# Another order of the first stage, a pool's mean ahead of a scheduling point, and one preparation step behind a product

## The chip, the cores and the metric

The kernel runs on one core of one Trainium2 chip. The metric is the time of one execution in microseconds, measured on the device; lower is better. Three executions of the kernel before took 1081.11, 1081.81 and 1083.24 us, a median of 1081.81 us.

## The reference

One layer of a hybrid decoder block on x of 1024 tokens by 1024 channels, all in float32: an RMSNorm, one projection `h @ w_in` whose columns are the queries and keys of four heads of differential attention, their values v, a multiscale trailing mean ("pool") and a gated short convolution; the output projection with a residual; then a second RMSNorm, a SwiGLU feed-forward layer of 2816 hidden channels with a residual, and a last RMSNorm.

```python
h = rmsnorm(x, g_mix[l]);  proj = h @ w_in[l]
q, k, v, p, gb, gc, hin = jnp.split(proj, list(split_pts), axis=-1)
att = diff_attention(q1, q2, k1, k2, vh, rel_bias, lam)
att = rmsnorm(att, subln_g[l], SUBLN_EPS) * (1.0 - lam_init)
pool = multiscale_pool(p, w_pool[l], pool_scale[l])
conv = short_gated_conv(gb, gc, hin, conv_w[l])
x = x + (jnp.concatenate([att, pool, conv], axis=-1) @ w_o[l])
h = rmsnorm(x, g_ffn[l])
x = x + (jax.nn.silu(h @ w_gate[l]) * (h @ w_up[l])) @ w_down[l]
return rmsnorm(x, g_final)
```

The multiscale pool is, per group of 64 channels, the mean over the last 2, 4, 8 or 16 tokens minus the token itself, times a small matrix.

## The kernel before

Every product is done in three passes of a split number: ACT writes a rounded high half (`nc.scalar.copy`), DVE the rest (`tensor_sub`), and PE multiplies high by high, low by high and high by low (`PASSES`). So nearly every operand passes through ACT and then DVE before PE can use it (`split_exact` L48, `halves_of` L136).

The tokens are worked in two halves, c = 0 and c = 1, of 512. The **first stage** (L186 to L379) loads x transposed, in four tiles of 256 channels for each half, and the weights of v, of k and of q. For c = 0 it does not wait for the norm: h is x times the gain, and the factor 1/rms of a token ("rstd") is put on behind the products. That factor comes from `squares` (ACT, L231), `square_sum` (DVE adds them, and for the last tile splits the total into two halves, L235), `token_rstd` (eight small PE products against ones, L255; a DVE step L259, a GpSimd power L261 and a DVE copy `rep` L263) and `along` (four PE transposes L269 and an ACT copy, `rbc`). `v_out` (L198) takes v of a block of 128 tokens from PSUM with rstd on it: twice an ACT step (L209) and a DVE step (L210). For c = 1, `normalise` (L275) makes the true h: DVE multiplies (`hn`, L288), then the two halves are split off (L50, L51). PE then does the products of v for c = 1 (`v_products`, L226). `of_gained` (L338) are the products of k and of q for c = 0, 24 matmuls each.

In this stage and in two others the program's text sets the order of the instructions on PE, ACT, DVE and GpSimd (`manual_schedule`); elsewhere a scheduler orders them, and may fill PE's order with products of the next part (L560: k and q for c = 1). Each engine takes its instructions in that order, and an instruction that waits holds up all behind it. PSUM banks come from three tags with two banks each: v of c = 0 has "c" and "f"; q's products take the "f" bank that `v_out(0, 2)` empties, and the v products of c = 1 need both "c" banks, emptied by `v_out(0, 0)` and `v_out(0, 1)`.

After this, `chain` (L530) runs the other columns of `w_in` while attention is worked between them. The pool's part is a generator, `windows` (L489): sums over windows, two `yield`s, the mean and its halves `ph` and `pl`, a `yield`, and the products (L523). At each `yield` other work is put in.

In the feed-forward layer, `unit(m, name)` (L1064) is one of seven products of a fast 2 by 2 scheme; M6, M7 and M4 add into one bank of the tag "f", which DVE reads in between (L1085, L1087, L1096). `prepare(m, part)` (L864) readies weights: part 1 is four DVE sums (L876 to L879).

Of the kernel before, what the change touches and what calls it, by code (L numbers as in the profile page):

```python
# [71 lines left out]
def tile_hybrid_block(ctx, tc, x, g_mix, w_in, lq1, lk1, lq2, lk2, subln_g, rel_bias, w_pool,  # L72
# [50 lines left out]
    def bank(tag, shape=(P, 512)):  # L123
        return psp.tile(list(shape), F32, tag=tag, name="ps_" + tag)
# [11 lines left out]
    def halves_of(raw, shape, pin=False, eng=nc.vector):  # L136

        hi = sl.new("w_hi", shape, F32R)
        lo = sl.new("w_lo", shape, F32R)
        ins = nc.scalar.copy(hi, raw)  # L140
        if pin:
            tc.keep_in_program_order(ins)
        eng.tensor_sub(lo, raw, hi.bitcast(F32))  # L143
        sl.done(raw)
        return hi, lo
# [76 lines left out]
    def v_products(c, n, ps, tbs=range(4)):  # L222
        w = wv[n // 2]
        for tb in tbs:
            for j, (a, b) in enumerate(PASSES):
                ins = nc.tensor.matmul(ps[tb], h[c][b][:, n, tb * P:(tb + 1) * P], w[a][:, n % 2, :],  # L226
                                       start=n == 0 and j == 0, stop=n == KT - 1 and j == 2)
                if c == n == j == 0:
                    tc.keep_in_program_order(ins)

    def squares(c, kk):  # L231
        sq = sqs[c, kk] = sl.new("sq", PAIR_SHAPE)
        nc.scalar.activation(sq, xt[c, kk], AF.Square)
# [68 lines left out]
    for kk in range(KT // 2):  # L302
# [9 lines left out]
        if kk < KT // 2 - 1:  # L312
            square_sum(0, kk)
            for k in range(2):
                v_products(0, 2 * kk + k, v_ps)
    squares(1, 0)
    kq_ws.append(halves_of(kq_raw[0], W_SHAPE))
    square_sum(0, KT // 2 - 1)
    squares(1, 1)
    squares(1, 2)  # L320
    squares(1, 3)
    v_products(0, KT - 2, v_ps)
    square_sum(1, 0)
    square_sum(1, 1)
    stat_ps = bank("a", (P, 2, 512))
    r0, rep0 = token_rstd(0, sums[0], stat_ps[:, 0, :])
    v_products(0, KT - 1, v_ps)
    square_sum(1, 2)
    rbc0 = along(rep0, stat_ps[:, 1, :])
    square_sum(1, 3)  # L330
    kq_ws.append(halves_of(kq_raw[1], W_SHAPE))
    k_ps = bank("a")

    def of_gained(w, ps, ks=range(KT)):

        for k in ks:
            for j, (a, b) in enumerate(PASSES):
                nc.tensor.matmul(ps, w[a][:, k, :], h[0][b][:, k, :], start=k == 0 and j == 0,  # L338
                                 stop=k == KT - 1 and j == 2)

    def scaled(ps):
        t = sl.new("scaled", (P, 512))
        nc.vector.tensor_mul(t, ps, rbc0)
        return t

    of_gained(kq_ws[0], k_ps, range(4))
    for tb in (2, 3):
        v_out(0, tb, v_ps[tb], r0[:, tb:tb + 1])
    stat_ps = bank("a", (P, 2, 512))
    r1, rep1 = token_rstd(1, sums[1], stat_ps[:, 0, :])  # L350
    of_gained(kq_ws[0], k_ps, range(4, KT))
    v_out(0, 0, v_ps[0], r0[:, :1])
    rbc1 = along(rep1, stat_ps[:, 1, :])

    def first_half(dones):

        k = scaled(k_ps)
        ps = bank("f")
        of_gained(kq_ws[1], ps)
        normalise(((1, 0),), {1: rbc1})  # L360
        v_out(0, 1, v_ps[1], r0[:, 1:2])
        dones[0](0, k)
        q = scaled(ps)
        dones[1](0, q)
        sl.done(k, q)
        normalise(((1, 1), (1, 2), (1, 3), (0, 0), (0, 1)), {0: rbc0, 1: rbc1})
        v1_ps = [bank(tag) for tag in "ccfa"]
        for n in range(KT - 2):
            v_products(1, n, v1_ps)
        for tbs in (2, 3), (0, 1):  # L370
            for n in range(KT - 2, KT):
                v_products(1, n, v1_ps, tbs)
            for tb in tbs:
                v_out(1, tb, v1_ps[tb], None)
            if tbs == (2, 3):
                normalise(((0, 2), (0, 3)), {0: rbc0})
        sl.done(rbc0, rbc1)
        for w in wv:
            sl.done(*w)  # L379
# [101 lines left out]
    def pool_columns(n):  # L481
        st = {}

        def done_p(c, ps):
            if "p" not in st:
                st["p"] = sl.new("pt")
            nc.scalar.copy(st["p"][:, c * 512:(c + 1) * 512], ps)

        def windows():  # L489
            pt = st["p"]  # L490
            sums = []
            src, length = pt, 1
            while len(sums) < (2, 4)[n]:
                w2 = sl.new("win")
                rows = slice(64 if len(sums) == (1, 3)[n] else 0, P)
                nc.vector.tensor_copy(w2[rows, :length], src[rows, :length])
                nc.vector.tensor_add(w2[rows, length:], src[rows, length:], src[rows, :-length])
                sums.append(w2)
                if len(sums) > 2:
                    sl.done(sums[-3])  # L500
                src = w2
                length *= 2
            yield
            yield
            mean = sl.new("mean")
            for half, src in enumerate(sums[-2:]):
                rows = slice(64 * half, 64 * half + 64)
                nc.vector.tensor_mul(src[rows, :16], src[rows, :16], inv[rows, n, :])
                nc.vector.scalar_tensor_tensor(out=mean[rows], in0=src[rows], scalar=1.0 / (2, 4, 8, 16)[2 * n + half],
                                               in1=pt[rows], op0=ALU.mult, op1=ALU.subtract)  # L510
            sl.done(*sums[-2:])
            src = mean
            ph = sl.new("ph", dt=F32R)
            pl = sl.new("pl", dt=F32R)
            split_exact(nc, ph, pl, src, nc.vector)
            sl.done(src)
            yield
            m = pt
            for c in range(2):
                half = slice(c * 512, (c + 1) * 512)  # L520
                ps = bank("f")
                for j, (a, b) in enumerate(PASSES):
                    nc.tensor.matmul(ps, wpool[:, a, n, :], (ph, pl)[b][:, half], start=j == 0, stop=j == 2)  # L523
                nc.scalar.activation(m[:, half], ps, AF.Copy, scale=pscale[:, n:n + 1])
            sl.done(ph, pl)
            spill(4 + n, m)

        return [column(P0 + n * P, done_p, windows)]
# [647 lines left out]
    for m in range(len(steps)):  # L1176
        unit(m, "M6")
        unit(m, "M5")
        if m > 2:
            prepare(m + 1, 0)  # L1180
        prepare(m + 1, 1)
        unit(m, "M7")
        prepare(m + 1, 2)
        if m > 3:
            unit(m, "M2")
        if 4 <= m + 1 < len(steps):
            unit(m + 1, "M1")
        unit(m, "M4")
        prepare(m + 1, 3)
        unit(m, "M3")  # L1190
        fetch(m + 2)
        if m % 2 == 0:
            down_sums(m // 2)
# [179 lines left out]
```

## Time and profile before

| what | value |
|---|---|
| median of three executions | 1081.81 us |
| the profiled execution, its own time | 1084.07 us |
| its span | 1082.3 us (1.8 us lie around it) |
| PE busy | 1058.5 us, 98% |
| DVE busy | 748.1 us, 69% |
| ACT busy | 462.4 us, 43% |
| PE's share of the chain that ended last | 76% |
| HBM traffic | 141 GB/s over the span |

PE is busy for 98% of the span, so the time is PE's work plus the few places where PE waits, plus the stretches in which its granted clock was lower. The granted clock was 0.992 of full over the whole execution. The three execution times and the profiled one differ by up to 2.96 us.

### The profile page before, as it was taken

What the parts mean: (1) busy time and instruction counts of PE and PEld (TensorE: products, weight loads), DVE (VectorE), ACT (ScalarE), POOL (GpSimd) and SP (SyncE); (2) the same over time, 40 slices, a digit from 0 to 9 for tenths busy, and PEclk for the clock granted to TensorE, in tenths of its full rate; (3) what the DMA queues carried; (4) which work ended last, traced back from release to release, by engine and by line L of the source; (5) the groups of instructions that cost most, each with busy time, mean ns of one, the idle gap of its engine ahead of it and who ended that gap; (6) DMA issues with size and microseconds to landing.
All of it is one profiled execution on the core that took longest, in us unless ns stands there. A gap on an engine that the chain in (4) does not pass through costs nothing.

```text
span 1082.3 us, 13281 instructions
## 1 busy us (share of the span) xinstructions
PE 1058.5 (98%) x4935; PEld 874.2 (81%) x4935; DVE 748.1 (69%) x1273; ACT 462.4 (43%) x813; POOL 32.6 (3%) x60
## 2 busy tenths in 40 slices
PE   9999999999999999999999999999999999999997
PEld 8777878887887878778888888888888888888886
DVE  6676767667787655878877766867777657565654
ACT  7445753657554436632332323323232334343442
POOL 0000000000000000000000000000000000000010
PEclk9999989999999999999999999999999999999999
DMA  8012021111252341226635545543544996476653
GB/s 273 1 48 69 21 58 60 59 40 59 78 185 97 126 138 59 83 94 213 214 107 178 172 129 174 193 163 111 175 167 152 319 360 216 138 223 205 199 178 129
DMA packets 100001, 153.20 MB, mean 142 GB/s; under 512 B 8504, under 2 KB 50016, under 8 KB 99936
## 3 DMA queue, kind: packets, MB, share of 16 engines
q1 hardware_dynamic: 99936, 152.35, 42.4%
q8 instruction: 39, 0.64, 0.2%
q14 instruction: 26, 0.21, 0.1%
HBM read 109.07 MB, written 44.05 MB: 141 GB/s over the span
## 4 chain that ended last, share of the span: by engine, by line
PE 76%; DVE 10%; ACT 5%; DMA 3%; issue 1%; POOL 0%; SPq 0%; POOLq 0%; ACTq 0%; DVEq 0%
PE ps_f L1074 17%; PE ps_a L1074 11%; PE ps_c L1074 10%; PE ps_a L1220 9%; PE ps_f L388 7%; PE ps_c L1220 5%; PE ps_f L785 5%; PE ps_f L1220 5%; PE ps_f L401 2%; PE ps_c L698 2%; ACT e L669 1%; DMA x<-raw 1%; PE ps_c L685 1%; PE ps_f L560 1%; DVE e L673 1%
## 5 line engine op out<-in xcount | busy, mean ns | idle before, releaser
L51 DVE TENSOR_TENSOR lo<-raw,hi 128x1024 fp32r<-128x1024 f32 (+1 forms) x84 | 93.4, 1134 | 76.7 <-ACT hi L50 70.8
L50 ACT CAST hi<-raw 128x1024 fp32r<-128x1024 f32 (+1 forms) x84 | 82.1, 982 | 118.5 <-DMA raw<-in_w_down 27.9
L1074 PE MATMUL ps_c<-b,w 128*128 128x512 f32 x528 | 124.1, 390 | 0.0
L388 PE MATMUL ps_f<-h,w_hi 128*128 128x512 f32 x384 | 123.0, 401 | 0.2 <-ACT w_hi L140 0.2
L1074 PEld LDWEIGHTS ps_c<-b,w 128*128 128x128 f32 x528 | 98.8, 188 | 21.0 <-ACT top L1091 0.4
L388 PEld LDWEIGHTS ps_f<-h,w_hi 128*128 128x128 f32 x384 | 70.9, 191 | 13.6 <-ACT w_hi L140 0.6
L388 PE MATMUL ps_f<-h,w_lo 128*128 128x512 f32 x192 | 76.3, 398 | 0.5 <-DVE w_lo L143 0.5
L785 PE MATMUL ps_f<-wo_hi,mix 128*128 128x512 f32 x224 | 75.4, 400 | 1.2 <-ACT mix L50 0.6
L51 DVE TENSOR_TENSOR w<-raw,w 128x512 fp32r<-128x512 f32 x66 | 45.1, 689 | 42.9 <-ACT w L50 42.8
L50 ACT CAST w_hi<-s 128x1024 fp32r<-128x1024 f32 x44 | 46.3, 1054 | 54.3 <-DVE s L878 46.9
L1074 PE MATMUL ps_f<-T,w 128*128 128x512 f32 x264 | 65.2, 397 | 1.9 <-DVE low L1087 1.9
L50 ACT CAST w<-raw 128x512 fp32r<-128x512 f32 x66 | 40.8, 623 | 59.0 <-PE ps_f L1074 25.8
L669 ACT ACTIVATE e<-ps_a,m 128x128 f32<-128x128 f32 (+7 forms) x64 | 47.1, 741 | 41.1 <-DVE m L666 38.3
L1074 PEld LDWEIGHTS ps_f<-T,w 128*128 128x128 f32 x264 | 50.5, 192 | 13.3 <-issue 2.3
L51 DVE TENSOR_TENSOR w_lo<-s,w_hi 128x1024 fp32r<-128x1024 f32 x44 | 53.7, 1220 | 9.8 <-DMA kept4S<-sum 2.7
L112 POOL TENSOR_TENSOR rstd<-ms,nhalf 128x1 f32<-128x1 f32 x48 | 28.7, 599 | 967.6 <-DVE ms L105 946.8
L1220 PE MATMUL ps_a<-lo,hi 128*128 128x512 f32 (+1 forms) x154 | 57.6, 374 | 0.0
L1220 PE MATMUL ps_a<-hi,lo 128*128 128x512 f32 (+1 forms) x154 | 57.6, 374 | 0.0
L1220 PE MATMUL ps_a<-hi 128*128 128x512 f32 (+1 forms) x154 | 57.5, 374 | 0.0
L1074 PE MATMUL ps_f<-t,w_hi 128*128 128x512 f32 x176 | 54.9, 390 | 1.1 <-ACT t L50 0.6
L1074 PE MATMUL ps_a<-t,w_hi 128*128 128x512 f32 x176 | 54.5, 389 | 0.0
L1074 PE MATMUL ps_a<-t3b,w_hi 128*128 128x512 f32 x176 | 54.2, 389 | 0.0
(245 smaller groups left out, 2297.9 us busy)
## 6 DMA issues: line engine op xcount, KB each, us to landing
raw<-in_w_down SPq DMA_DIRECT2D x37, 512.0 KB, 4.5
raw<-in_w_gate SPq DMA_DIRECT2D x23, 512.0 KB, 6.0
raw<-in_w_up SPq DMA_DIRECT2D x23, 512.0 KB, 4.0
raw<-in_w_in SPq DMA_DIRECT2D x19, 512.0 KB, 4.2
raw<-in_w_o SPq DMA_DIRECT2D x8, 512.0 KB, 4.0
raw<-in_x SPq DMA_DIRECT2D x8, 512.0 KB, 3.8
x<-raw SPq DMA_DIRECT2D x8, 512.0 KB, 2.7
x<-x SPq DMA_DIRECT2D x8, 512.0 KB, 6.7
```

The lines of the kernel that those rows point to most:

```text
L50: nc.scalar.copy(hi, src)
L51: lo_eng.tensor_sub(lo, src, hi.bitcast(F32))
L112: nc.gpsimd.tensor_tensor(r, ms, nhalf, op=ALU.pow)
L388: nc.tensor.matmul(ps, w[a][:, k, :], h[c][b][:, k, :], start=k == 0 and j == 0, stop=k == KT - 1 and j == 2)
L401: nc.tensor.matmul(ps, w[a][:, k, :], h[c][b][:, k, :], start=k == 0 and j == 0, stop=k == KT - 1 and j == 2)
L560: nc.tensor.matmul(ps, w[a][:, k, :], h[1][b][:, k, :], start=k == 0 and j == 0, stop=k == KT - 1 and j == 2)
L669: nc.scalar.activation(es[:, :n], ps[:, :n], AF.Exp, bias=m[:, 1:2], scale=-1.0, accum_out=z[:, s:s + 1])
L673: nc.vector.scalar_tensor_tensor(out=e[0][:, :n], in0=e[1][:, :n], scalar=t, in1=e[0][:, :n], op0=ALU.mult, op1=ALU.add)
L698: nc.tensor.matmul(av[:, :(2 - a) * DV], pts[j // 4][:, a, (j % 4) * P:(j % 4 + 1) * P], rhs, start=j == 0 and a == 0, stop=j == i and a == 1)
L785: nc.tensor.matmul(wo_ps[t][nh], halves[m, t // 4][:, a, cols], wo[m][b][:, nh * 512:(nh + 1) * 512], start=m == SET_A[0] and j == 0, stop ...
L1074: nc.tensor.matmul(ps, w[a][:, k, :], h[b][k], start=new and k == 0 and j == 0, stop=k == 3 and j == 2, skip_group_check=not new)
L1220: nc.tensor.matmul(ps, a_op[a][:, j, i * P:(i + 1) * P], b_op[b][:, j, cols], start=start and p == 0, stop=stop and p == 2, skip_group_che ...
```

## The change

Three edits. In the first stage the four squares of c = 1 stand on ACT ahead of the sum's halves of c = 0, all sums of c = 1 ahead of `token_rstd(0)`, the second `token_rstd` ahead of the exits of v, and the exits of v follow later, mixed with `normalise`, which now makes all of h in one go; the last v products go (3, 2) before (0, 1). In the pool, one of the two `yield`s between the window sums and the mean stands between the mean and its halves. In the feed-forward loop, `prepare(1, 1)` follows `unit(0, "M7")` where it stood ahead of it.

```diff
--- before.py
+++ after.py
@@ -313,22 +313,19 @@
             square_sum(0, kk)
             for k in range(2):
                 v_products(0, 2 * kk + k, v_ps)
-    squares(1, 0)
-    kq_ws.append(halves_of(kq_raw[0], W_SHAPE))
+    for kk in range(KT // 2):
+        squares(1, kk)
     square_sum(0, KT // 2 - 1)
-    squares(1, 1)
-    squares(1, 2)
-    squares(1, 3)
-    v_products(0, KT - 2, v_ps)
     square_sum(1, 0)
     square_sum(1, 1)
+    kq_ws.append(halves_of(kq_raw[0], W_SHAPE))
+    v_products(0, KT - 2, v_ps)
+    square_sum(1, 2)
     stat_ps = bank("a", (P, 2, 512))
+    square_sum(1, 3)
     r0, rep0 = token_rstd(0, sums[0], stat_ps[:, 0, :])
     v_products(0, KT - 1, v_ps)
-    square_sum(1, 2)
     rbc0 = along(rep0, stat_ps[:, 1, :])
-    square_sum(1, 3)
-    kq_ws.append(halves_of(kq_raw[1], W_SHAPE))
     k_ps = bank("a")
 
     def of_gained(w, ps, ks=range(KT)):
@@ -344,36 +341,37 @@
         return t
 
     of_gained(kq_ws[0], k_ps, range(4))
-    for tb in (2, 3):
-        v_out(0, tb, v_ps[tb], r0[:, tb:tb + 1])
     stat_ps = bank("a", (P, 2, 512))
     r1, rep1 = token_rstd(1, sums[1], stat_ps[:, 0, :])
+    kq_ws.append(halves_of(kq_raw[1], W_SHAPE))
+    v_out(0, 2, v_ps[2], r0[:, 2:3])
     of_gained(kq_ws[0], k_ps, range(4, KT))
-    v_out(0, 0, v_ps[0], r0[:, :1])
     rbc1 = along(rep1, stat_ps[:, 1, :])
+    v_out(0, 3, v_ps[3], r0[:, 3:4])
 
     def first_half(dones):
 
+        normalise(((1, 0),), {1: rbc1})
+        for tb in (0, 1):
+            v_out(0, tb, v_ps[tb], r0[:, tb:tb + 1])
         k = scaled(k_ps)
         ps = bank("f")
         of_gained(kq_ws[1], ps)
-        normalise(((1, 0),), {1: rbc1})
-        v_out(0, 1, v_ps[1], r0[:, 1:2])
+        normalise(((1, 1),), {1: rbc1})
         dones[0](0, k)
         q = scaled(ps)
+        normalise(((1, 2),), {1: rbc1})
         dones[1](0, q)
         sl.done(k, q)
-        normalise(((1, 1), (1, 2), (1, 3), (0, 0), (0, 1)), {0: rbc0, 1: rbc1})
+        normalise(((1, 3), *((0, kk) for kk in range(KT // 2))), {0: rbc0, 1: rbc1})
         v1_ps = [bank(tag) for tag in "ccfa"]
         for n in range(KT - 2):
             v_products(1, n, v1_ps)
-        for tbs in (2, 3), (0, 1):
+        for tbs in (3, 2), (0, 1):
             for n in range(KT - 2, KT):
                 v_products(1, n, v1_ps, tbs)
             for tb in tbs:
                 v_out(1, tb, v1_ps[tb], None)
-            if tbs == (2, 3):
-                normalise(((0, 2), (0, 3)), {0: rbc0})
         sl.done(rbc0, rbc1)
         for w in wv:
             sl.done(*w)
@@ -501,7 +499,6 @@
                 src = w2
                 length *= 2
             yield
-            yield
             mean = sl.new("mean")
             for half, src in enumerate(sums[-2:]):
                 rows = slice(64 * half, 64 * half + 64)
@@ -509,6 +506,7 @@
                 nc.vector.scalar_tensor_tensor(out=mean[rows], in0=src[rows], scalar=1.0 / (2, 4, 8, 16)[2 * n + half],
                                                in1=pt[rows], op0=ALU.mult, op1=ALU.subtract)
             sl.done(*sums[-2:])
+            yield
             src = mean
             ph = sl.new("ph", dt=F32R)
             pl = sl.new("pl", dt=F32R)
@@ -1178,8 +1176,11 @@
         unit(m, "M5")
         if m > 2:
             prepare(m + 1, 0)
-        prepare(m + 1, 1)
+        if m:
+            prepare(m + 1, 1)
         unit(m, "M7")
+        if not m:
+            prepare(1, 1)
         prepare(m + 1, 2)
         if m > 3:
             unit(m, "M2")
```

The first stage on DVE. `sq` are the squares and their sums, `ssum` the total's low half, `stat` and `rep` the steps of the rstd, `w_lo` the low halves of k's and q's weights, `v<-ps_f` and `v<-ps_c` the exits of v (blocks 2 and 3, 0 and 1), `hn` and `h` the second half's h. Before:

```order
L51 TENSOR_TENSOR ssum<-sq,ssum 128x512
L241 TENSOR_TENSOR sq<-sq 128x1024
L595 TENSOR_TENSOR rb<-rb_612,rb 32x4
L622 TENSOR_SCALAR sub_640<-sub_640 128x1
L259 TENSOR_SCALAR stat_296<-ps_a 128x4
L263 COPY rep<-stat_296 128x512
L241 TENSOR_TENSOR sq<-sq 128x1024 x2
L246 TENSOR_TENSOR sq<-sq 128x512
L51 TENSOR_TENSOR ssum<-sq,ssum 128x512
L143 TENSOR_TENSOR w_lo<-raw,w_hi 128x1024
L210 SCALAR_TENSOR_TENSOR v<-ps_f,stat_296,v 128x2x128 x4
L259 TENSOR_SCALAR stat_361<-ps_a 128x4
```

And after:

```order
L51 TENSOR_TENSOR ssum<-sq,ssum 128x512
L241 TENSOR_TENSOR sq<-sq 128x1024
L143 TENSOR_TENSOR w_lo<-raw,w_hi 128x1024
L241 TENSOR_TENSOR sq<-sq 128x1024 x2
L246 TENSOR_TENSOR sq<-sq 128x512
L51 TENSOR_TENSOR ssum<-sq,ssum 128x512
L259 TENSOR_SCALAR stat_302<-ps_a 128x4
L263 COPY rep<-stat_302 128x512
L259 TENSOR_SCALAR stat_347<-ps_a 128x4
L263 COPY rep<-stat_347 128x512
L143 TENSOR_TENSOR w_lo<-raw,w_hi 128x1024
L210 SCALAR_TENSOR_TENSOR v<-ps_f,stat_302,v 128x2x128 x4
```

The first `rep` stood between the sums of the second half; now it stands behind all of them, and both `rep` stand ahead of the weights' second `w_lo` and the exits.

The pool of the columns 128 to 255 on ACT, during attention. `ph` is the high half of the mean, `att` the copies by which attention's result leaves PSUM, `q` and `u` the exits of projections, `pT` and `e` parts of attention, `w_hi` a weight's high half. Before:

```order
L669 ACTIVATE e,z<-ps_a,m 128x1024 x2
L687 CAST pT<-ps_c 128x512
L687 CAST pT<-ps_c 128x384
L421 ACTIVATE q<-ps_f 64x512
L50 CAST ph<-mean 128x1024
L702 ACTIVATE att<-ps_c,z 128x128
L721 ACTIVATE att<-ps_c,sub_640 128x128
L669 ACTIVATE e,z<-ps_a,m 128x128
L450 COPY u<-ps_f 128x512
L120 ACTIVATE junk,ss<-att 128x128
L669 ACTIVATE e,z<-ps_a,m 128x128
L140 CAST w_hi<-raw 128x1024
```

And after:

```order
L700 ACTIVATE att<-ps_c,z 128x128
L719 ACTIVATE att<-ps_c,sub_640 128x128
L50 CAST ph<-mean 128x1024
L120 ACTIVATE junk,ss<-att 128x128
L419 ACTIVATE q<-ps_f 64x512
L667 ACTIVATE e,z<-ps_a,m 128x1024 x2
L685 CAST pT<-ps_c 128x512
L685 CAST pT<-ps_c 128x384
L419 ACTIVATE q<-ps_f 64x512
L448 COPY u<-ps_f 128x512
L140 CAST w_hi<-raw 128x1024
L700 ACTIVATE att<-ps_c,z 128x128
```

`ph` moved ahead by one block of attention; `u` and `w_hi`, which stood behind the `att` copies, now stand ahead of them.

The start of the feed-forward loop on DVE. `T` are halves of an operand, `low<-ps_f` is the read of M7's bank (L1087 before, L1085 after), `s` the sums of `prepare(1, 1)`. Before:

```order
L51 TENSOR_TENSOR T_4415<-turned,T_4413 128x2x128
L876 TENSOR_TENSOR s<-raw 128x512
L1087 TENSOR_TENSOR low<-ps_f,low 128x512
L877 TENSOR_TENSOR s<-raw,s 128x512
L1088 TENSOR_TENSOR low<-ps_a,low 128x512
L878 TENSOR_TENSOR s<-s,raw 128x512
```

And after:

```order
L51 TENSOR_TENSOR T_4415<-turned,T_4413 128x2x128
L1085 TENSOR_TENSOR low<-ps_f,low 128x512
L874 TENSOR_TENSOR s<-raw 128x512
L1086 TENSOR_TENSOR low<-ps_a,low 128x512
L875 TENSOR_TENSOR s<-raw,s 128x512
L51 TENSOR_TENSOR w<-raw,w 128x512
L876 TENSOR_TENSOR s<-s,raw 128x512
```

The read of the bank moved ahead of the first `s`.

## Rows read from the trace of the kernel before

**Rows 1.** Who PE waited for, whole span: total us, times, longest us.

```profile
PE ps_c L685 <- ACT att L721: 3.4, 4, 2.3
PE ps_a L269 <- DVE rep L263: 2.1, 1, 2.1
PE ps_f L1074 <- DVE low L1087: 1.9, 1, 1.9
PE ps_a L658 <- DVE v L51: 1.3, 1, 1.3
PE ps_c L226 <- DVE h L51: 0.7, 1, 0.7
...
PE ps_c L226 <- ACT h L50: 0.5, 1, 0.5
```

**Rows 2.** Stretches: length, busy PE PEld DVE ACT POOL, PEclk, DMA share, GB/s.

```profile
41.40:44.70 3.30, 3.30 (x9) 2.52 (x9) 2.19 (x5) 1.31 (x3) 0.00 (x0) 0.50 0.01 2
72.00:75.40 3.40, 2.05 (x11) 1.45 (x10) 2.52 (x7) 1.02 (x3) 0.00 (x0) 1.00 0.00 0
...
147.20:153.90 6.70, 5.93 (x18) 4.96 (x19) 5.26 (x12) 4.38 (x13) 0.54 (x1) 0.50 0.00 0
...
474.90:478.20 3.30, 3.30 (x9) 2.52 (x9) 3.30 (x6) 1.88 (x2) 0.00 (x0) 0.50 0.42 140
```

**Rows 3.** The tile xt, 16 to 17 us: last loads of x, issue and landing.

```profile
L174 SPq DMA_DIRECT2D xt<-in_x_t x2: 471/1705/2939, 13.6 to 16.6; - x2
...
DMA to landing us min/median/max: 9.7/9.7/9.7
```

**Rows 4.** Timeline of ACT, first stage: start, length, instruction, [idle before, releaser].

```profile
24.11 0.62 ACT L50 CAST ssum<-sq 128x512 fp32r<-128x512 f32 x1 [3.16 <-DVE sq L246]
24.64 2.95 ACT L233 ACTIVATE sq<-xt 128x1024 f32<-128x1024 f32 x3
```

**Rows 5.** Timeline of DVE, first stage.

```profile
29.54 2.55 DVE L241 TENSOR_TENSOR sq<-sq 128x1024 f32<-128x1024 f32 x2
...
33.57 0.69 DVE L51 TENSOR_TENSOR ssum<-sq,ssum 128x512 fp32r<-128x512 f32 x1 [0.75 <-ACT ssum L50]
34.51 1.23 DVE L143 TENSOR_TENSOR w_lo<-raw,w_hi 128x1024 fp32r<-128x1024 f32 x1 [0.25 <-ACT w_hi L140]
...
36.67 0.88 DVE L210 SCALAR_TENSOR_TENSOR v<-ps_f,stat,v 128x256 fp32r<-128x256 f32 x2 [0.54 <-ACT v L209]
...
39.77 0.43 DVE L263 COPY rep<-stat 128x512 f32<-128x512 f32 x1 [1.13 <-POOL stat L261]
...
42.14 1.41 DVE L288 SCALAR_TENSOR_TENSOR hn<-xt,gm,rbc 128x512 f32<-128x512 f32 x2
```

**Rows 6.** Timeline of PE, first stage.

```profile
26.84 0.95 PE L255 MATMUL ps_a<-ones,ssum 128*128 128x2 f32 x8
...
30.52 0.60 PE L269 MATMUL ps_a<-ident,rep 128*128 128x128 f32 x4
...
34.31 0.94 PE L255 MATMUL ps_a<-ones,ssum 128*128 128x2 f32 x7 [0.44 <-DVE ssum L51]
...
40.67 0.70 PE L338 MATMUL ps_f<-h,w_hi 128*128 128x512 f32 x2
...
47.80 1.52 PE L226 MATMUL ps_c<-wv,h 128*128 128x512 f32 x6
```

**Rows 7.** Timeline, 143 to 149 us: the pool's mean and what waits.

```profile
143.73 2.45 DVE L509 SCALAR_TENSOR_TENSOR mean<-win,pt 64x1024 f32<-64x1024 f32 x2
...
146.22 1.04 ACT L50 CAST ph<-mean 128x1024 fp32r<-128x1024 f32 x1 [4.60 <-DVE mean L509]
...
147.97 1.12 PE L685 MATMUL ps_c<-ident,e 128*128 128x128 f32 x4 [2.29 <-ACT att L721]
```

**Rows 8.** Timeline of DVE, 473 to 475 us.

```profile
473.20 0.68 DVE L876 TENSOR_TENSOR s<-raw 128x512 f32<-128x512 f32 x1
473.80 0.68 DVE L1087 TENSOR_TENSOR low<-ps_f,low 128x512 f32<-128x512 f32 x1
```

## The prediction

> **What bounds the kernel now.** The table of engines says that PE is busy for 98% of the span, so I read next whom PE waits for [rows 1], then the granted clock around the longest of these waits [rows 2], then the timelines of ACT, DVE and PE at these places [rows 3 to 8]. The reader is to see that a wait of PE costs twice. It costs its own length, and where it is long enough the clock falls right behind it to 1.2 of 2.4 GHz: PEclk reads 0.50 behind the wait of 2.1 for `rep`, behind that of 2.3 for `att` and behind that of 1.9 for `low`, and 1.00 around the wait of 1.3 for v [rows 1, 2]. At half the clock, half of PE's busy time is lost: 3.30/2 = 1.65 us, 5.93/2 = 2.97 us and 3.30/2 = 1.65 us [rows 2]. So each of the three edits goes at one of the three costly places: 2.1 + 1.65 in the first stage, 2.3 + 2.97 at the pool, 1.9 + 1.65 in the feed-forward loop.
>
> **First stage, the first sums.** Order decides here, and ACT is the engine to follow. The last tile of x is issued at 16.6 and lands 9.7 later, at 26.3 [rows 3]. ACT's cast of c = 0's total (`ssum`, 0.62) ran at 24.11, ahead of that tile's square [rows 4]. Now it stands behind all four squares of c = 1, the last of which can start at 26.3 and takes 2.95/3 = 0.98. Cast 0.62, low half on DVE 0.69 [rows 4, 5]: 26.3 + 0.98 + 0.62 + 0.69 = 28.6. PE's first sums ran at 26.84 without a wait [rows 6]; they start 1.8 later.
>
> **The first rstd.** On DVE the first `token_rstd` now stands behind all sums of c = 1 and one `w_lo`. From 28.6: one sum 2.55/2 = 1.28 and `w_lo` 1.23 make 31.1. The rest of c = 1's sums took from 29.54 to 33.57 + 0.69 = 34.26, that is 4.72, of which 0.75 was a wait for ACT [rows 5]; without or with it they end at 35.1 or 35.8. The rstd then takes a small step, 1.13 for the power and 0.43 for `rep` [rows 5], about 1.7: 36.8 to 37.5, and I take 37.1. PE comes to these transposes at 28.6 + (30.52 - 26.84) = 32.3 [rows 6], and waits 4.8, longer than any of the waits behind which the clock fell. I count one fall of the size of the first stage's own, 1.65. It is the same price as before, only earlier, so the gain in clock that the edit could bring here is nil.
>
> **The second rstd and q.** From the transposes to the end of the second sums PE took 34.31 + 0.94 - 30.52 = 4.73, of which 0.44 was a wait [rows 6] that falls away, as the sums are ready by then. So they end at 37.1 + 4.29 + 1.65 = 43.0. DVE has been idle since 37.1, some 6 us: the reason is that `w_lo` and the exits, which filled this time, now stand behind the second `rep`. From 43.0: rstd 1.7, `w_lo` 1.23, exit of block 2 two DVE steps of 0.48 (the pair took 0.88) with 0.54 of ACT between [rows 5], 1.5: 47.4. PE without a wait would be at q by 43.0 + (40.67 - 35.25 - 2.13) = 46.3, where 35.25 is the second sums' end and 2.13 the old wait for `rep`, to the hundredth of the timeline (2.1 in [rows 1]; the others in [rows 6]). But q's products take the bank that the exit of block 2 empties, so q starts at 47.4, against 40.67. Its 24 products took 47.80 - 40.67 = 7.13 [rows 6] with the 1.65 in them; at full clock 5.48: 52.9 against 47.80, 5.1 late.
>
> **The exits of blocks 0 and 1.** Ahead of them DVE has block 3's exit (1.5), `hn` 1.41 [rows 5], and the halves of h: ACT's cast of 128x1024, taken from `ph`, 1.04 [rows 7], and the low half, taken from `w_lo`, 1.23: 47.4 + 1.5 + 1.41 + 1.04 + 1.23 = 52.6. Two exits of 1.5 end at 54.1 and 55.6. The second half's v products need both banks. PE is there at 52.9, so it waits about 1.6 and then, after one block's product, 0.8 (bounds 0 and 3.0 for both, which is their whole length): 7.5 late. Against this, the waits for h (0.7 and 0.5) and the last v (1.3) [rows 1] go, since h now runs ahead: 5.0 late. What is late next: all eight pieces of h on ACT and DVE now stand ahead of the last exits and of the exits of k and q for attention. The trace of before does not show this; from below it costs 0, from above two waits like the 1.3 and the 1.9 that it shows elsewhere, 3.2 [rows 1]. I take 1.5, near one such wait. The first stage: +6.5, with 5.0 - 2.4 + 0 = +2.6 and 5.0 + 0.6 + 3.2 = +8.8 as its ends. The moved weight loads on SP cost nothing: PE works on q for 5.5 us and v for longer before the pool's products use them.
>
> **The pool.** ACT stood 4.60 us at the head of its queue with `ph`, which waited for two means of 2.45 us in all, and the `att` copy behind it kept PE for 2.29 [rows 7]. With a scheduling point between mean and halves, `ph` comes one block of attention after the mean and does not stand any more. What is late next: a copy `u` of 128x512 (0.62 for a cast of this size [rows 4]) and a `w_hi` (1.04 for one of its size) are now ahead of an `att` copy, 1.66 together. I let PE wait 1.4 there, a little less than they last: -0.9. Such a wait is next to the 1.3 without a fall, so the 2.97 go. The mean itself now stands 2.45 earlier on DVE among attention's steps: 0 if DVE's gaps (31% of the span) take it, 2.45 if PE waits for all of it; I take 0.7, nearer to nothing. Sum -0.9 - 2.97 + 0.7 = -3.2. The ends: -2.29 - 2.97 = -5.3, and 0 - 0 + 0.7 = +0.7, where the wait stays and the clock falls as before. The other pool's mean had no long wait of PE beside it (the four of that kind make 3.4 in all, with 2.3 in this one [rows 1]): nothing.
>
> **The feed-forward loop.** `s` (0.68) ran ahead of the read of M7's bank, and the read began 0.60 after it [rows 8]; PE waited 1.9 and lost 1.65 behind it. With the read first the wait is 1.9 - 0.6 = 1.3, the length that left the clock at 1.00 around 73 us [rows 1, 2]. Sum: -0.6 - 1.65 = -2.25, ends -1.9 - 1.65 = -3.55 (all of the wait gone) and 0. The moved `s` has the products of M7 and of the next unit as cover; without that it would give the 0.6 back.
>
> **The sum.** +6.5 - 3.2 - 2.25 = +1.05 us. On the profiled execution (1084.07: the span of 1082.3 and 1.8 around it) that makes 1085.1; that execution is 2.26 above the median of 1081.81, as the three runs themselves lie 2.1 apart, so on the median it is 1082.9.
>
> **Rivals.**
> Slower: the new waits of 1.4 to 1.6 us are just over the point at which the clock falls. They are PE's waits for the exit of block 0 near 54 us, for attention's first products near 85 us, and for `att` near 150 us. For it: the trace has 1.3 without a fall and 1.9 with one, and 1.6 is between. Against it: 1.3 is as near. What decides is where between the two the clock begins to fall. One fall costs 1.65: 1084.5; two, 1086.2; the pool's fall staying as it was, 2.97: 1085.9.
> The Trainium skill (TensorE: Matmul & The Clock Gate, section "Part 1: The HAM clock gate") has a rule on this side: the gate runs on its own time, so that the number of slow matmuls differs between runs of the same kernel. By it a wait is no sure sign either way, and the 2.97 and the 1.65 counted as gains need not come back in each run, up to 4.6 on top of the sum. The one profile here fits it, with 1.3 and 1.9 on the two sides, but cannot test it.
>
> Faster: the exits of blocks 0 and 1 are ready in time (ACT and DVE get through `normalise` and the exits beside q's products) and nothing new is late behind h: -2.4 - 1.5 = -3.9, so 1079.0. For it: DVE is idle 31% of the span. Against it: in this stretch its queue has no gap after 43 us by the sum above.
>
> As the first words of the change have it: the first stage loses its waits and falls (2.13 + 1.65 + 1.2 + 1.3 = 6.3) and gains no new one, beside -5.45 of the other two: 1070.1. Against it stands the landing of x at 26.3 [rows 3], which no order moves, and that the first `rep` is behind more work.
>
> **How the numbers follow.** Forecast 0.47 (own range 1080.5 to 1084.2), slower rival 0.37, faster rival 0.13, the last 0.03. 0.2% of the median is 2.16 us, about what a measurement of this kernel can tell from no change. The forecast lies within it for nearly all its range. Faster: 0.13 of the faster rival less its part above 1079.6, the 0.03, and a little of the forecast, 0.16. Slower: nearly all of its rival and the top of the forecast, 0.38. Same: 0.46. The range goes from the faster rival's 1079.0 to 1086.4, past two falls.
>
> **What would show it.** In the changed kernel's trace: PE waiting about 1.8 for `ssum` near 28.6 and 4.8 for `rep` near 37; a PEclk of 0.50 in some 3 us behind it and full clock during q; DVE idle some 6 us between the two `rep`; waits for an exit of v near 47 and 54 to 56; no wait for h and for the last v as long as before; near 150 us no idle ACT ahead of `ph` and PEclk 1.00; near 475 us PEclk 1.00. Wrong would make it a first `rep` before 33 us, an unbroken half clock behind the pool or the loop's start, or more than one fall in the first 90 us.

## The result, and the profile after

The changed kernel took 1090.7 us (median of four executions, 1089.15 to 1092.68), against 1082.3 us of the kernel before on the same chip (1081.11 to 1083.24): a ratio of 1.0079, 95% interval 1.0059 to 1.0100. In a second set of runs the ratio was 1.0066 (1.0046 to 1.0086). So the change costs 7 to 8.5 us, where +1.05 was forecast, and the range ended at 1086.4. The profiled execution took 1091.29 us, its span is 1089.5 us.

Whom PE waited for in the changed kernel, over the whole span (total us, times, longest us), to be read against [rows 1]:

```profile
PE ps_a L269 <- DVE rep L263: 4.7, 1, 4.7
PE ps_c L683 <- ACT att L719: 2.0, 3, 1.1
PE ps_c L226 <- DVE v L210: 1.7, 2, 1.2
PE ps_f L1072 <- DVE low L1085: 1.5, 2, 1.3
PE ps_f L386 <- ACT w_hi L140: 1.5, 1, 1.5
...
PE ps_f L558 <- DVE v L51: 1.1, 1, 1.1
PE ps_f L335 <- DVE v L210: 1.0, 1, 1.0
...
PE ps_a L656 <- DVE v L51: 0.9, 1, 0.9
```

The waits are nearly those of the forecast: 4.7 for the first `rep` (4.8), 1.0 for the exit ahead of q (1.1), 1.2 and 0.5 for the next exits (1.6 and 0.8), 1.1 and 0.55 for `att` (1.4), 1.3 for `low` (1.3); the old waits for h and for the second `rep` are gone. New and not in the sum is the 1.5 for `w_hi`, near 262 us. The granted clock is another matter. Stretches of the changed kernel, columns as in [rows 2]:

```profile
34.80:41.80 7.00, 5.68 (x16) 4.61 (x17) 0.43 (x1) 1.91 (x3) 0.80 (x1) 0.51 0.00 0
86.00:93.00 7.00, 7.00 (x17) 4.05 (x16) 2.42 (x5) 2.80 (x6) 0.00 (x0) 0.51 0.11 16
153.95:160.80 6.85, 5.25 (x33) 4.22 (x32) 4.36 (x13) 3.86 (x12) 0.54 (x1) 1.00 0.00 1
478.20:482.00 3.80, 2.46 (x12) 1.73 (x11) 3.80 (x11) 0.62 (x1) 0.00 (x0) 1.00 0.84 259
```

The pool (third line) and the loop (fourth) run at full clock, as forecast. But the fall at the first `rep` lasts twice as long as counted (half of 5.68 is 2.8 us, not 1.65), and there is a second one from 86 to 93 us, in which half of 7.00, 3.5 us, is lost. Just ahead of it PE waits twice, for the last exits of v:

```profile
83.82 0.30 PE L656 MATMUL ps_a<-k,q 128*128 128x128 f32 x1 [0.95 <-DVE v L51]
...
85.32 0.70 PE L558 MATMUL ps_f<-h,w_hi 128*128 128x512 f32 x2 [1.09 <-DVE v L51]
```

Why DVE is late all through the first stage is to be seen in its timeline, against [rows 5]:

```profile
35.64 0.43 DVE L263 COPY rep<-stat 128x512 f32<-128x512 f32 x1 [1.22 <-POOL stat L261]
42.94 0.16 DVE L259 TENSOR_SCALAR stat<-ps_a 128x4 f32<-128x4 f32 x1 [6.88 <-PE ps_a L255]
44.23 0.43 DVE L263 COPY rep<-stat 128x512 f32<-128x512 f32 x1 [1.13 <-POOL stat L261]
44.58 1.22 DVE L143 TENSOR_TENSOR w_lo<-raw,w_hi 128x1024 fp32r<-128x1024 f32 x1
45.71 0.48 DVE L210 SCALAR_TENSOR_TENSOR v<-ps_f,stat,v 128x256 fp32r<-128x256 f32 x1
```

First PE waits 4.7 us for DVE; then DVE waits 6.88 us for PE's second sums, with `w_lo` and the exits queued behind its small step. The two engines take turns.

### The profile page after: what moved, and what is told of

It reads as the page before. It is cut to its first block, busy times and chain, and to the rows that moved or that the text cites. A ratio compares the mean times of both kernels' runs of the same rounds, so it can differ in the third digit from the quotient of the medians.

```text
span 1089.5 us, 13282 instructions
## 1 busy us (share of the span) xinstructions
PE 1059.7 (97%) x4935; PEld 873.5 (80%) x4935; DVE 747.2 (69%) x1273; ACT 461.7 (42%) x813; POOL 33.6 (3%) x60
## 4 chain that ended last, share of the span: by engine, by line
PE 70%; DVE 14%; ACT 5%; DMA 4%; issue 2%; SPq 0%; POOL 0%; POOLq 0%; ACTq 0%; DVEq 0%
PE ps_f L1072 13%; PE ps_a L1221 9%; PE ps_c L1072 8%; PE ps_f L386 8%; PE ps_a L1072 8%; PE ps_c L1221 6%; PE ps_f L1221 5%; PE ps_f L783 5%; PE ps_c L696 2%; PE ps_f L399 2%; DMA raw<-in_w_gate 1%; ACT e L667 1%; PE ps_c L683 1%; PE ps_a L657 1%; PE ps_a L656 1%
## 5 line engine op out<-in xcount | busy, mean ns | idle before, releaser
L1072 PE MATMUL ps_f<-t3b,w_hi 128*128 128x512 f32 x176 | 54.5, 391 | 0.5 <-DVE top L1083 0.5
```

What stands on the lines that cost most here:

```text
L1072: nc.tensor.matmul(ps, w[a][:, k, :], h[b][k], start=new and k == 0 and j == 0, stop=k == 3 and j == 2, skip_group_check=not new)
```

## The experiments

The ratios below are to the kernel before on the same chip, with 95% intervals. 0.001 is 1.08 us.

**The parts alone.** Kernel before with the first stage's edit only (`stage_only`, and `stage_again` for one more profile); with the pool's only (`mean_only`); with the loop's only (`loop_only`); with both of these (`mean_loop`). The edits are the hunks of the diff shown above.

> Only the first stage's edit, the pool and the loop as before. Theory A: the first stage alone costs what the two others give back and the net loss on top, 8.4 + 5.5 = 13.9 us over before, some 1096, with the fall of the clock behind the waits near 84 and 85 us (0.95 and 1.09 us in the changed kernel) again. Rival B (the fall near 86 us was chance in the profiled run): 10 us or less, some 1092, with no fall there.

> The first stage as before, only the pool's and the loop's edit. Theory A (the pool's and the loop's gains hold, the whole loss is the first stage's): PE waits under 1.5 us at both places, granted clock 1.00 there, 5.5 us under before (3.3 for the pool, 2.2 for the loop), some 1077. Rival B (the clock's falls are a matter of the run, and come back elsewhere): between 1080 and 1083.

> The kernel before with the pool's edit alone. Theory A (the edit wins 0.7 us of wait and what the falls of the clock cost on average, loses 0.8 at the weight near 254 us): waits of 1.0 and 0.6 where 2.3 stood, 1.5 for w_hi near 254, and 0.5 to 2 us under before. Rival B (the full sum of the prediction for this place): 3.2 us under before.

> The kernel before with the loop's edit alone. Theory A: the wait of 1.9 is 1.3, no fall of the clock behind it, and 0.6 to 1.7 us under before. Rival B (nothing beyond the wait's 0.6, the fall comes in few runs): within 0.7 us of before.

| kernel | ratio | in us | forecast for this part |
|---|---|---|---|
| first stage | 1.0081 (1.0062 to 1.0101) | +8.8 (6.7 to 10.9) | +6.5 (2.6 to 8.8) |
| pool | 0.9987 (0.9975 to 0.9999) | -1.4 (-2.7 to -0.1) | -3.2 (-5.3 to +0.7) |
| loop | 0.9990 (0.9979 to 1.0002) | -1.1 (-2.3 to +0.2) | -2.25 (-3.55 to 0) |
| pool and loop | 0.9984 (0.9974 to 0.9995) | -1.7 (-2.8 to -0.5) | -5.45 |

The first stage costs more than forecast, the other two bring less than half of it (for the loop alone the interval still holds its forecast; for both together it does not). Within their intervals the parts add up: 8.8 - 1.7 = 7.1, with the two sets of the whole change at 7.1 and 8.5. For `stage_only` both theories were off: its 8.8 is under A's 13.9, since the pool and the loop had less to give, and no fall came near 86 us in its profile. For `mean_loop` neither 1077 nor 1080 to 1083 was hit; 1079.63 lies between. Theory A holds for `mean_only`; for `loop_only` the number is A's too, but its interval does not separate the two theories. In `mean_only` the waits behind the pool are 1.05 and 0.55 for 2.29; at the second pool's weight PE now waits 1.5 where before it waited 0.18 and 0.53:

```profile
145.93 0.66 PE L685 MATMUL ps_c<-ident,e 128*128 128x128 f32 x4 [1.05 <-ACT att L721]
147.13 0.63 PE L685 MATMUL ps_c<-ident,e 128*128 128x128 f32 x4 [0.55 <-DVE att L703]
```

```profile
PE ps_f L388 <- ACT w_hi L140: 1.5, 1, 1.5
```

**Is a fall of the clock part of a kernel?** The kernel before and the changed one were profiled again, unaltered.

> The kernel before unaltered, one more profile. Theory A (falls behind waits near 2 us vary by the run): the same waits (2.1, 2.3, 1.9) within 0.1, but fewer or shorter stretches at half clock than the 3.4, 6.8 and 3.4 us of the first profile, so that pool and loop had less to give back than 2.97 + 1.65. Rival B: the same three stretches.

> The changed kernel unaltered, to see what differs between its runs. Theory A (the falls of the clock behind waits of 1 to 2 us are a matter of the run; only the one behind the 4.7 us wait comes each time): the waits for rep, for the exits of v, for att and for low within 0.1 of those of the first profile, but no fall near 86 us; median 1088 to 1091. Rival B (the fall near 86 us belongs to this kernel's waits): the fall at 86 is there again.

> The changed kernel unaltered, a third profile. Theory A (the two waits near 84 and 85 us, each about 1.0, together let the clock fall): both again at 0.9 or more, and half clock behind them. Rival B (chance): the same two waits and no fall.

> The first stage's edit alone, a second profile. In the first one the earlier of the two waits near 84 us was 0.33 and no fall came. Theory A: a fall if the earlier wait is about 1.0 this time, none if it is 0.3 again; at the pool, where PE waits 2.3, a fall again; at the loop, where it waits 1.9, a fall in about one of two. Rival B (no relation): a fall with 0.3 or none with 1.0.

The waits at the forecast's places, for `rep`, the exits, `att` and `low`, repeat to about 0.1 us (where the clock fell a little earlier, that for the first `rep` was 3.1 to 3.3, as PE was slower to come to it); those for `ssum` (0.45 to 1.6) and, near 84 us, for v (0.33 to 1.14) do not, and neither do the falls. In the second profile of before (1082.32 us) the wait of 2.2 near 40 us had none behind it, but waits of 1.45 and 0.65 for h near 55 us had one of 3.4, and that of 2.3 at the pool one of 3.4 us for 6.8. In the second of the changed kernel (1087.70 us) the fall near 86 us was there, which spoke for its rival B; the third decided otherwise. A stretch of the changed kernel's third profile (1086.42 us), behind waits of 1.14 and 1.10, and one of the second profile of the first stage alone (1091.59 us), behind 0.99 and 1.10:

```profile
85.00:93.00 8.00, 8.00 (x34) 5.78 (x33) 3.01 (x6) 3.96 (x9) 0.00 (x0) 1.00 0.29 97
```

```profile
86.00:93.00 7.00, 7.00 (x17) 4.08 (x16) 2.42 (x5) 2.83 (x7) 0.00 (x0) 0.51 0.05 12
```

In 8.00 us PE ran 34 matmuls, in 7.00 us of the other execution 17, with the same waits ahead. So rival B of `after_third` (chance) holds, and theory A falls as a rule for each execution. In the five profiles with this first stage there was a fall near 86 us in three; of the two without, one is this third profile, the other (`stage_only`) had waits of 0.33 and 1.10. `rstd_first`, below, has the pair of waits again, and a fall from 79.6 to 83.1:

```profile
77.99 0.30 PE L656 MATMUL ps_a<-k,q 128*128 128x128 f32 x1 [1.07 <-DVE v L51]
79.50 1.06 PE L558 MATMUL ps_f<-h,w_hi 128*128 128x512 f32 x2 [1.09 <-DVE v L51]
```

Over all the profiles taken, for the places of the forecast and for these:

| wait of PE | profiles | us at half clock, from within the wait or just behind it |
|---|---|---|
| `rep`, 4.1 to 4.7 | 6 | 6.8 in each |
| `rep`, 3.1 to 3.3, with 3.4 us at half clock ahead of it | 2 | 3.4 in each |
| pool, 2.3 | 5 | 6.8, 3.4, 3.4, 3.4, 3.4 |
| pool, 0.8 to 1.1 and 0.55 | 12 | 3.4 in one, none in eleven |
| second `rep`, 2.1 to 2.2 | 5 | 3.4, 3.4, none in three |
| loop, 1.9 | 5 | 3.4, 3.4, none in three |
| loop, 1.3 | 12 | none |
| h, 1.45 to 2.3 and then 0.65 | 5 | 3.4, 3.4, 3.4, none in two |
| v, 0.95 to 1.14 and then 1.1 | 5 | 6.8, 6.8, 3.4, 3.4, none |
| the same two, 0.33 to 0.84 and 0.5 to 1.1 | 3 | none |

So one execution's fall is a draw, but the share of executions that fall goes with the waits: all at 2.3 and at 4 and more, two of five at 1.9 to 2.2, four of five at two waits of about 1, none of twelve at a single one of 1.3. What decides in one execution is not shown.

The loop with its wait of 1.9, in the first profile of the first stage alone, and the stretch behind it, which stays at 1.00 where [rows 2] had 0.50:

```profile
479.55 2.97 PE L1072 MATMUL ps_f<-T,w 128*128 128x512 f32 x12 [1.94 <-DVE low L1085]
```

```profile
479.50:486.00 6.50, 6.45 (x29) 5.37 (x30) 6.50 (x10) 3.06 (x3) 0.00 (x0) 1.00 0.47 151
```

**Which move of the first stage costs.** Each of two moves was undone alone in the changed kernel, and both together.

> The changed kernel with the weights' second low half and three exits of v put ahead of the second rstd, into the 6.9 us in which DVE had nothing to do. Theory A (the second half of the first stage's loss is this idle stretch, which delays everything on DVE): the waits for the exits (1.04 + 1.23 + 0.46) go, a wait of about 1.3 for the second rep comes, the waits near 84 us come 2 to 3 us earlier; 3 to 5 us under the changed kernel, some 1086. Rival C (DVE is behind all the same from 50 us on): within 1.5 us of the changed kernel.

```diff
-    r1, rep1 = token_rstd(1, sums[1], stat_ps[:, 0, :])
     kq_ws.append(halves_of(kq_raw[1], W_SHAPE))
-    v_out(0, 2, v_ps[2], r0[:, 2:3])
+    for tb in (2, 3, 0):
+        v_out(0, tb, v_ps[tb], r0[:, tb:tb + 1])
+    r1, rep1 = token_rstd(1, sums[1], stat_ps[:, 0, :])
...
-    v_out(0, 3, v_ps[3], r0[:, 3:4])
...
-        for tb in (0, 1):
-            v_out(0, tb, v_ps[tb], r0[:, tb:tb + 1])
+        v_out(0, 1, v_ps[1], r0[:, 1:2])
```

> The changed kernel with the first rstd put ahead of the last two sums of c = 1; the exits of v stay behind the second rstd. Theory A (the order of the exits on DVE is the larger half of the loss): the wait for the first rep falls from 4.7 to about 0.5, but the second sums wait about 1 and the v products of c = 1 wait about 2.6 and 0.8 for the exits, so that 3 us at most are won: 1085 to 1088. Rival B (the wait of 4.7 us and the fall of the clock behind it are the loss): 5 to 7 us won, some 1083.

```diff
-    square_sum(1, 2)
     stat_ps = bank("a", (P, 2, 512))
-    square_sum(1, 3)
     r0, rep0 = token_rstd(0, sums[0], stat_ps[:, 0, :])
     v_products(0, KT - 1, v_ps)
+    square_sum(1, 2)
+    square_sum(1, 3)
```

> The changed kernel with both moves undone at once: the first rstd ahead of the last two sums of c = 1, and w_lo and three exits ahead of the second rstd. Theory A (the two moves are one loss, DVE's 6.9 idle microseconds, and each alone takes most of it back: 5 to 7 us): little is left to win for the second, 1080 to 1083, no wait over 1 us for an exit, but one of 2 to 3 for the second rep near 45 us. Rival B (they add up, 7 + 5 us): under 1078.

`exits_first`: 1.0007 (0.9997 to 1.0018), `rstd_first`: 1.0022 (1.0007 to 1.0038), `both_undone`: 1.0007 (0.9995 to 1.0020). Against the whole change's 1.0066 to 1.0079, each alone takes 5 to 8 us back, and both together no more than `exits_first` alone. The first stage's loss is not gone with that: the three kernels keep the pool's and the loop's edits, which alone stand at 0.9984, so that 2.5 us of it remain in two of them and 4.1 in `rstd_first`, and which of the other moves costs these is not shown. Theory A of `exits_first` holds (more was won than its 3 to 5, and the second `rep` waits 0.53 for its 1.3); for `rstd_first` its rival B is right, with 1083.77 us for "some 1083", and the waits of 2.6 and 0.8 that A counted for the exits were 1.17 and 0.46. PE's waits in `exits_first`, and in `rstd_first`:

```profile
37.04 1.12 PE L269 MATMUL ps_a<-ident,rep 128*128 128x128 f32 x4 [4.67 <-DVE rep L263]
46.96 0.66 PE L269 MATMUL ps_a<-ident,rep 128*128 128x128 f32 x4 [0.53 <-DVE rep L263]
81.57 0.30 PE L655 MATMUL ps_a<-k,q 128*128 128x128 f32 x1 [0.84 <-DVE v L51]
82.76 0.70 PE L557 MATMUL ps_f<-h,w_hi 128*128 128x512 f32 x2 [0.50 <-DVE v L51]
```

```profile
31.55 0.66 PE L269 MATMUL ps_a<-ident,rep 128*128 128x128 f32 x4 [0.19 <-DVE rep L263]
...
41.35 0.76 PE L335 MATMUL ps_f<-h,w_hi 128*128 128x512 f32 x2 [1.08 <-DVE v L210]
48.31 0.96 PE L226 MATMUL ps_c<-wv,h 128*128 128x512 f32 x3 [1.17 <-DVE v L210]
```

With the exits in DVE's gap the 4.67 stays, and with it 6.8 us at half clock, but nothing waits for an exit any more until 81 us. Not all of the gap was ready work: `w_lo`, put first, waited 2.81 there itself for ACT's `w_hi`. With the first rstd early the 4.7 goes and the waits for the exits stay. With both, one wait of 4.07 for the second `rep` takes their place, since that step now stands behind `w_lo` and three exits:

```profile
43.77 1.12 PE L269 MATMUL ps_a<-ident,rep 128*128 128x128 f32 x4 [4.07 <-DVE rep L263]
```

This is theory A of `both_undone`, with 1083.05 us at the edge of its 1080 to 1083 and a wait of 4.07 for its 2 to 3. So the two moves are one loss: either one undone takes most of it back, and undoing the other as well brings nothing more than `exits_first`.

**h between the last exits again, and work in place of a wait.**

> The changed kernel with the last two pieces of h put back between the two pairs of v's exits, where before had them. Theory A (the waits near 84 and 85 us come from all of h standing ahead of the last exits): the two waits merge or shrink, no fall of the clock there, 3 to 5 us under the changed kernel, some 1086. Rival C (what is late there is DVE's queue as a whole, since its work begins 5 us late and has no gap from 43 to 82 us): the wait only moves to the next use of v, as the 1.3 us of before, and the time stays within 2 us of the changed kernel.

```diff
-        normalise(((1, 3), *((0, kk) for kk in range(KT // 2))), {0: rbc0, 1: rbc1})
+        normalise(((1, 3), (0, 0), (0, 1)), {0: rbc0, 1: rbc1})
...
+            if tbs == (3, 2):
+                normalise(((0, 2), (0, 3)), {0: rbc0})
```

> The changed kernel with twenty products of no use (128x512, 0.23 us each, 4.5 us) on PE in the place where it waits 4.7 us for the first rep; their bank is overwritten by the transposes behind them. The wait is replaced by work, nothing else is moved. Theory A (the fall of the clock at 35 to 42 us is the price of that wait, 1.6 to 3.4 us): clock 1.00 through the first stage, 1.5 to 3 us under the changed kernel, some 1087. Rival C (the next waits, of 1.0 and 1.2, let the clock fall instead, or DVE is the bound from 43 to 82 us and takes it back): within 1 us of the changed kernel.

```diff
     v_products(0, KT - 1, v_ps)
+    for _ in range(20):
+        nc.tensor.matmul(stat_ps[:, 1, :], wv[0][0][:, 0, :P], h[0][0][:, 0, :], start=True, stop=True)
     rbc0 = along(rep0, stat_ps[:, 1, :])
```

`tail_back`: 1.0075 (1.0058 to 1.0091), no gain; rival C holds. The two waits became one of 1.63 for v at 79 us, without a fall behind it in this profile, but attention's order shifted with them and had 2.9 us of other waits from 86 to 135 us, where before had 0.4 on the same stretch of work. `fill_wait`: 1.0070 (1.0053 to 1.0087) against 1.0066 of the changed kernel on the same chip, which is rival C's number. It settles little: the twenty products had to wait 1.84 themselves for the bank that DVE's small step was reading, and ended at 40.2, 3 to 4 us after the transposes of the changed kernel began (36.1 and 37.3 in two profiles). The clock was at full from 34.4 on, but there had been a fall from 31.0.

**Versions.** Of the first stage's moves one alone, the second rstd ahead of the exits of blocks 2 and 3, was put on top of the pool's and the loop's edits; then the exits were taken two blocks at a time.

> The pool's and the loop's edit, and of the first stage's one thing alone: the second rstd ahead of the exits of blocks 2 and 3 (squares, sums, h and the other exits as before). Theory A (that one move is good, what costs is the rest): no wait of PE for the second rep (2.1 before), at most 0.7 for the exit ahead of q, and 2 to 4 us under the kernel with the pool's and the loop's edit alone (1079.6), some 1076.5. Rival C (the exits come later and the waits move to the v products of c = 1 near 46 us, up to 2.7 us in all): 1079 to 1081.

```diff
-    for tb in (2, 3):
-        v_out(0, tb, v_ps[tb], r0[:, tb:tb + 1])
     stat_ps = bank("a", (P, 2, 512))
     r1, rep1 = token_rstd(1, sums[1], stat_ps[:, 0, :])
+    for tb in (2, 3):
+        v_out(0, tb, v_ps[tb], r0[:, tb:tb + 1])
```

> The pool's and the loop's edit, the second rstd ahead of the exits of v as in the kernel with that move alone, and the exits taken two blocks at a time (first halves of both, then second halves), so that ACT and DVE don't take turns on one bank; blocks 0 and 1 stand behind the first piece of h. Theory A (the turns of 0.54 us each are what keeps the exits late): the waits of 0.8 and 0.7 at 44 to 47 us go, and 1 to 2 us under the kernel with the move alone (1079.4), some 1078. Rival C (PE is only earlier at the next piece of h, near 54 us, and waits there up to 2.6): 1079 to 1080.

```diff
-    def v_out(c, tb, ps, scale):
+    def v_out(c, tb, ps, scale, pairs=range(2)):
...
-        for pair in range(2):
+        for pair in pairs:
...
-    for tb in (2, 3):
-        v_out(0, tb, v_ps[tb], r0[:, tb:tb + 1])
     stat_ps = bank("a", (P, 2, 512))
     r1, rep1 = token_rstd(1, sums[1], stat_ps[:, 0, :])
+    for pair in range(2):
+        for tb in (2, 3):
+            v_out(0, tb, v_ps[tb], r0[:, tb:tb + 1], (pair,))
...
-    v_out(0, 0, v_ps[0], r0[:, :1])
...
+        normalise(((1, 0),), {1: rbc1})
+        for pair in range(2):
+            for tb in range(2):
+                v_out(0, tb, v_ps[tb], r0[:, tb:tb + 1], (pair,))
...
-        normalise(((1, 0),), {1: rbc1})
-        v_out(0, 1, v_ps[1], r0[:, 1:2])
```

`rstd1_ahead`: 0.9987 (0.9976 to 0.9997), level with `mean_loop` (0.9984): its rival C. The 2.1 for the second `rep` went, and PE waited at 38.4 (0.31), 45.5 (0.76), 46.9 (0.69) and for h near 55 (1.46 and 0.65). `paired_exits`: 0.9975 (0.9964 to 0.9986), 1078.74 us, the lowest ratio of the study, 2.7 us under before and 1.3 under `rstd1_ahead` by the ratios (their intervals overlap): A's gain, with C's wait. The waits of 0.76 and 0.69 are gone. In its timeline four exits take DVE 1.9 us without the turns of 0.54, and PE then waits for the next piece of h:

```profile
37.02 0.87 DVE L210 SCALAR_TENSOR_TENSOR v<-ps_f,stat,v 128x256 fp32r<-128x256 f32 x2
38.04 0.88 DVE L210 SCALAR_TENSOR_TENSOR v<-ps_f,stat,v 128x256 fp32r<-128x256 f32 x2 [0.15 <-ACT v L209]
```

```profile
54.04 0.50 PE L226 MATMUL ps_c<-wv,h 128*128 128x512 f32 x1 [2.26 <-ACT h L50]
```

## Why the prediction was wrong

The step that failed is the price of the clock, taken on both sides of the sum from the falls of one profile. As gains it counted 2.97 + 1.65 = 4.6 us, of which 2.6 were lost work on average; in the first stage it counted one fall of 1.65, where 2.8 us were lost at `rep` and 1.7 more on average near 86 us.

*The gains.* The pool was given -2.97 and the loop -1.65 for falls that one execution had shown, and this was put on the median of others. The prediction saw that the profiled execution stood 2.26 above the median and passed over it as scatter; the falls were part of that scatter. By the table above, half clock stands behind the pool's wait for 4.1 us on average (20.4/5) and behind the loop's for 1.4 (6.8/5), which is 2.0 and 0.7 us of lost work. With the waits' own change (2.29 to 1.05 + 0.55, and 1.94 to 1.34), the 0.14 that a fall in one of twelve still costs, and 1.5 - 0.7 = 0.8 more wait at the second pool's weight, this makes -0.7 - 2.0 + 0.1 + 0.8 = -1.8 for the pool and -0.6 - 0.7 = -1.3 for the loop. Measured alone they are -1.4 and -1.1, and both together -1.7 (-2.8 to -0.5), less than this estimate's -3.1. Lost work is not all lost time: from a copy of q on ACT ahead of the pool to a copy `u` behind it, `mean_only`, without a fall, took 21.60 us (131.00 to 152.60), the five executions with the pool as before 23.00 to 24.46, on average 1.8 more. With 0.7 of that for the wait, the falls cost 1.1 here, not 2.0.

*The losses.* The first stage's waits came out 1.7 us lower than forecast in the first profile: lower at the first sums (0.45, and up to 1.6 in another execution, for 1.8; the last tile of x landed at 25.3 in the first profile, not at the 26.3 of [rows 3]) and at the exits (1.7 for 2.4; the sum's own terms, the exit's end at 54.1 and PE's arrival at 52.9, give 1.2 where it put 1.6, and 1.23 was measured), higher near 84 us (2.0 for 1.5). But its clock was counted as one fall of 1.65, equal to before's. The five profiles of this stage have 6.8 us at half clock around the first `rep`, in the first of them 2.8 us of lost work, so 1.2 more; three of the five have 3.4 to 6.8 us near 86 us, 3.4 on average over the five, 1.7 us of lost work. So 6.5 - 1.7 + 1.2 + 1.7 = 7.7, and 8.8 was measured. More than one fall in the first 90 us was also the prediction's own sign of being wrong.

What the falls cost in time is seen from one step that every execution has, the same copy of q on ACT during attention. In `mean_only`, `after_third` and the first profile of the changed kernel:

```profile
131.00 0.60 ACT L421 ACTIVATE q<-ps_f 64x512 fp32r<-64x512 f32 x1 [2.10 <-DVE q L422]
```

```profile
138.16 0.59 ACT L419 ACTIVATE q<-ps_f 64x512 fp32r<-64x512 f32 x1 [2.10 <-DVE q L420]
```

```profile
142.15 0.59 ACT L419 ACTIVATE q<-ps_f 64x512 fp32r<-64x512 f32 x1 [2.10 <-DVE q L420]
```

With the first stage of before it comes at 131.0 to 132.2 us in five executions, 131.7 on average. With the changed one it comes at 138.2 and 138.6 where the clock did not fall near 86 us, at 140.7 where it fell for 3.4 us, and at 142.2 twice where it fell for 6.8: 140.4 on average, 8.6 later. So the loss arises before this step, the first stage without the fall near 86 costs 6.4 to 6.9, close to the forecast's 6.5, and that fall brings the rest. The closeness is in part luck, as lower waits (-1.7) and the longer fall at `rep` (+1.2) nearly cancel.

In the first stage of before the clock fell in three profiles of five only, and its fall behind the second `rep` cost little. The next piece of h starts 15.20 us behind that wait's end with the fall (`before`, 40.26 to 55.46) and 15.21 without (`mean_only`, 40.14 to 55.35): PE, at half clock, only waits less for it.

```profile
55.46 0.50 PE L226 MATMUL ps_c<-wv,h 128*128 128x512 f32 x1 [0.46 <-ACT h L50]
```

```profile
55.35 0.50 PE L226 MATMUL ps_c<-wv,h 128*128 128x512 f32 x1 [1.45 <-ACT h L50]
```

*The rivals.* The slower rival named the mechanism and the place (a fall behind new waits near 85 us), with a wrong condition. It looked for a length of wait between 1.3 and 1.9 at which the clock falls; but waits of 1.94 were followed by none in three executions of five, and 1.0 with 1.1 by one in four of five. Its price of 1.65 was that of the shortest fall. The rule of the Trainium skill that stood behind it (TensorE: Matmul & The Clock Gate, section "Part 1: The HAM clock gate"), that the slow matmuls of one kernel differ in number between runs, is what the runs show, in the middle of a kernel too: 1.00 and 0.51 behind the same waits. The prediction put the gain that need not come back at up to 4.6 us; by the lost work 2.0 of it did not on average (2.97 - 1.9 and 1.65 - 0.7).

*The edit costed at nothing.* The second pool's mean was said to cost nothing; PE waits 0.8 us more for the weight `w_hi` behind it on ACT.

What stays open: how the two sets of the whole change (8.5 and 7.1 us) differ, as their intervals overlap; what decides in one execution whether a wait of 1 to 2 us is followed by a fall; and which other moves of the first stage cost the 2.5 us that stay with both moves undone.

## What to carry to other kernels

A fall of the clock seen in one profile is a draw: before it is counted as a gain, compare the profiled execution with the median, and count it at the share of profiles that show it. What it costs is read from when a later step comes, since PE may wait less behind a fall. Before a small step that waits for another engine is moved ahead on an in-order engine, look at what it then holds up: here a step of 0.16 us stood at the head of DVE's queue for 6.88 us with `w_lo` and the exits behind it, and putting these ahead of it took 6 to 8 us back. And two moves that fill the same gap are worth one of them, so undo them singly and together.

## What the runs showed of the hardware that had not been expected

Executions of one program differ in their falls of the clock: the three profiled executions of the changed kernel took 1091.29, 1087.70 and 1086.42 us, with two falls of 6.8 us in the first, four of 3.4 in the second and two of 3.4 in the third (the tail's left out). The falls are only a part of what lies between them, as the first two have 13.6 us at half clock each and lie 3.6 apart. A wait of 3.1 us for the first `rep` in place of 4.7 was no gain, since PE had come to it later, at half clock.

Where ACT and DVE each took two pieces of one PSUM bank in turn, DVE stood 0.54 us between its two steps [rows 5]; taken alternately from two banks, the four steps needed 1.9 us with one gap of 0.15 (`paired_exits`).
